# Forming three of thirty-two groups of a tuned matmul with seven block products, in list-scheduled orders

## The chip, the cores and the metric

The kernel runs on one core of one Trainium2 chip. The metric is the device time of one execution in microseconds (us). The engines of the core are TensorE (PE, matmuls; PEld is its weight load), VectorE (DVE), ScalarE (ACT), GpSimd (POOL, which also issues the loads of x) and SyncE (SP, which issues nearly all stores). They run at the same time, each through its own list of instructions in order, and wait for one another by semaphores.

## The reference

```python
B, S, D = (16, 2048, 1024)
def reference(x, w, decay):        # x: B,S,D   w: D,D   decay: D, all float32
    xw = x @ w
    out[:, 0, :] = xw[:, 0, :]
    for t in range(1, S):
        out[:, t, :] = decay[None, :] * out[:, t - 1, :] + xw[:, t, :]
```

A matrix product of 32768 rows, followed by a linear recurrence over time with one decay for each output channel.

## The kernel before

**Tiles.** Time is cut into 64 chunks of 512 steps, two neighbouring chunks make a group of 1024 steps, and the 1024 output channels make 8 blocks of 128. A *tile* is one group and one block of channels; its product lies in PSUM as 128 channels x 1024 steps (two banks), so that the recurrence runs along the free axis. The reduction over 1024 inputs takes 8 steps k, for each of the two chunks: 16 matmuls of 128x512 in bf16 for a tile (line L131). A *slot* is one tile's turn on TensorE; 31 groups give 248 slots, and the last group is done as two chunks of 8 slots each. Three double-bank tiles `ps0` to `ps2` turn over in PSUM; `spare0` and `spare1` are two more banks, and `spare1` holds the squares of the decays.

**Before the product.** GpSimd's queue loads a chunk of x in four quarters as bf16 (`load`, L105, tile `xb`). VectorE transposes it in 32x32 blocks (`turn`, L115, `xw`), and ScalarE reorders it in two halves into the layout that TensorE streams (`part`, L123, `xt`, a ring of 5).

**After the product.** A tile is done in one of two ways. *Unpaired*: VectorE scans all 1024 steps straight out of PSUM (`run`, L221) into `so`. *Paired*: ScalarE copies the tile out of PSUM to `xs` (`copy`, L183) and makes decay times the even steps in `h` (`odd`, L169); GpSimd adds `h` to the odd steps (`join`, L196); VectorE scans only the 512 odd steps, with the squared decay (`scan`, L201); ScalarE makes decay times the odd results (`even`, L169); and GpSimd adds them to the even steps (`fill`, L246). In either case `save` (L250) keeps the last column where the next group continues the sequence, VectorE transposes the result back in 32x32 blocks (`back`, L258, tile `ot`, a ring of 4 that holds four tiles each), and once four tiles are there SyncE stores them (L282).

**Rings and orders.** `so` is a ring of 4 tiles, `xs` of 3, `h` of 4. The order of each engine's instructions is the program's order. For the first 34 slots and the last 20 it is written out by hand in the table `agenda`, a string of steps for each slot (p copy, g odd, z start value, j join, S scan, h even, c fill, k save, B back, T turn, X and Y part, L load). In between, `usual(s)` gives each slot the same pattern, and two of eight tiles are unpaired. In each slot s that is: the copy, odd half, start value and join of tile s if it is paired, the scan of tile s-1 (or of s itself if unpaired), even half, fill and save of s-1, the out-transpose of s-2 or s-1, then the transposes and parts due for later chunks (`later`), and one or two loads.

Of the kernel before, what the change touches and what calls it, by code (L numbers as in the profile page):

```python
# [25 lines left out]
def kernel(  # L26
# [26 lines left out]
    nc = tc.nc  # L53
# [13 lines left out]
    CH = D // 2  # L67
    CR = CH // NQ

    const = ctx.enter_context(tc.tile_pool(name="const", bufs=1))  # L70
# [23 lines left out]
    def ot_tile(nj):  # L94
        return ring(sb, "ot", 4, [128, nj, CR])

# [22 lines left out]
    def part(c, copy, m0, m1, j0=0, j1=NJ):  # L119
        if c not in xt_of:  # L120
            xt_of[c] = ring(sb, "xt", 5, [128, M, 2, TL], BF16)
        src = xw_of[c][:, m0:m1, j0:j1].rearrange("p m j i e -> p m e (j i)")
        pin(copy(out=xt_of[c][:, m0:m1, :, j0 * P:j1 * P], in_=src))  # L123
# [17 lines left out]
    class Tile:  # L141
# [3 lines left out]
        def __init__(self, g, n, ps, outlets):  # L145
            self.b, self.t0 = chunks[g[0]]
            self.T = TL * len(g)
            self.n, self.ps, self.outlets = n, ps, outlets
            self.paired = n % R != R - 1
            if len(tiles) in flips or len(tiles) - len(slots) in flips:  # L150
                self.paired = not self.paired
            self.turn = len(tiles)
            self.lot = sum(t.paired for t in tiles)
            self.prev = None if self.t0 == 0 else last[n]
            if self.t0 + self.T < S:
                last[n] = const.tile([128, 1], FP32, name=f"keep{n}", bufs=2)
                self.keep = last[n]
            else:
                self.keep = None

        @property
        def so(self):
            if not hasattr(self, "held"):
                self.held = sb.tile([128, 2 * TL + 2], FP32, name=f"so{self.turn % 4}")
            return self.held

        def decayed(self, src):
            h = ring(sb, "h", 4, [128, TL])[:, 0:self.T // 2]
            pin(nc.scalar.activation(  # L169
                out=h, in_=src, func=mybir.ActivationFunctionType.Copy,  # L170
                scale=dec[:, self.n:self.n + 1]))
            return h
# [8 lines left out]
        def copy(self):  # L181
            self.xs = sb.tile([128, 2 * TL], FP32, name=f"xs{self.lot % 3}")[:, 0:self.T]
            pin(nc.scalar.copy(out=self.xs, in_=self.ps))  # L183

        def odd(self):
            self.g = self.decayed(self.ps[:, 0:self.T:2])

        def zero(self):
            if self.prev is None:
                pin(nc.gpsimd.memset(self.so[:, 1:2], 0.0))  # L190
# [3 lines left out]
        def join(self):  # L194
            odds = self.xs[:, 1:self.T:2]
            pin(nc.gpsimd.tensor_tensor(out=odds, in0=self.g, in1=odds, op=ALU.add))  # L196

        def scan(self):
            T, n, so = self.T, self.n, self.so
            if self.paired:  # L200
                pin(nc.vector.tensor_tensor_scan(  # L201
                    out=so[:, 3:T + 2:2],
                    data0=squares[-1][:, n:n + 1].to_broadcast([128, T // 2]),
                    data1=self.xs[:, 1:T:2],
                    initial=0.0 if self.prev is None else self.prev,
                    op0=ALU.mult,
# [8 lines left out]
        def run(self, ps, t, size):  # L215
# [3 lines left out]
            else:  # L219
                before = 0.0 if self.prev is None else self.prev  # L220
            pin(nc.vector.tensor_tensor_scan(  # L221
# [12 lines left out]
        def complete(self):  # L234
            if self.paired:
                self.even()
                self.fill()
            if self.keep is not None:
                self.save()

        def even(self):
            self.h = self.decayed(self.so[:, 1:self.T + 1:2])

        def fill(self):
            T = self.T
            pin(nc.gpsimd.tensor_tensor(  # L246
                out=self.so[:, 2:T + 2:2], in0=self.h, in1=self.xs[:, 0:T:2], op=ALU.add))

        def save(self):
            pin(nc.scalar.copy(out=self.keep, in_=self.so[:, self.T + 1:self.T + 2]))  # L250

# [14 lines left out]
    class Outlet:  # L266


        def __init__(self, ns, nj, half=0, queues=(nc.sync,), pieces=1):
            self.pieces = pieces  # L270
            self.ns, self.missing, self.half = ns, set(ns), half
            self.nj, self.t0, self.queues = nj, half * nj * P, queues
            self.ot = ot_tile(nj)

# [133 lines left out]
    def turn_and_load(c):  # L408
# [60 lines left out]
        20: "Y7 S19 L c16 k17 h17 T8 k19 L c17",  # L469
        21: "p20 g20 L S18 X8 j20 B17 B19",  # L470
        22: "L h18 p21 c18 B16 k18 g21 B18 Y8 z20 L j21 S20",
        23: "p22 z21 z22 S21 L h20 g22 T9 c20 h21",
        24: "k21 k20 j22 S23 X9 L c21 Y9 B20 L",
        25: "B23 k23 p24 B21 g24 z24 j24 S22 z25",
        26: "p25 T10 k22 h22 g25 c22 S24 X10 j25",
        27: "B22 p26 S25 g26 z26 Y10 j26",
        28: "S27 h25 h24 c25 S26 c24",
# [26 lines left out]
    flips = (1, 13, 15, -19, -18, -11, -8, -6, -3, -2)  # L504
    later = {}
    begun = {"T": 12, "X": 11, "Y": 11}
    for c in range(5, nch):
        first = c // 2 * K
        ahead = (7, 6, 4) if c % 2 else (11, 10, 8)
        for letter, a in zip("TXY", ahead):  # L510
            if c >= begun[letter]:
                later.setdefault(first - a, []).append(f"{letter}{c}")

    def usual(s):
        paired = [t.paired for t in tiles]
        do = [f"P{s}"] if paired[s] else []
        if paired[s - 1]:
            do.append(f"S{s - 1}")
        if not paired[s]:
            do.append(f"S{s}")  # L520
        do.append(f"C{s - 1}")
        if paired[s - 2]:
            do.append(f"B{s - 2}")
        if not paired[s - 1]:
            do.append(f"B{s - 1}")
        return do + later.get(s, []) + ["L"] * (2 if len(loads) > NQ else 1)

    def rest(s):
        do = [f"S{s - 1}"] if tiles[s - 1].paired else []
        do.append(f"C{s - 1}")  # L530
        if tiles[s - 2].paired:
            do.append(f"B{s - 2}")
        return do + [f"B{s - 1}"] + later.get(s, []) + ["L"] * len(loads)

    def perform(do):
        for deed in do:
            deeds[deed[0]](int(deed[1:] or 0))

    perform(agenda[-99].split())
    spares = [spare] + [ring(psp, "spare1", 1, [128, TL])]  # L540
    for step, (g, n) in enumerate(slots):
        T = TL * len(g)
        left = step - len(slots)
        if n % R == 0:
            ns, nj = range(n, n + R), T // P
            both = -6 * R <= left < -2 * R
            outlets = [Outlet(ns, nj, queues=(nc.sync, nc.gpsimd) if both else (nc.sync,),
                              pieces=2 if left == -2 * R else 1)]
        if left == -R:
# [52 lines left out]
        tiles.append(Tile(g, n, ps, outlets))  # L602
        do = agenda.get(step, agenda.get(left) if left >= -20 else None)
        if do is None:
            do = usual(step)
        else:
            do = do.split()
            if left == -20:
                do = rest(step) + do
        perform(do)  # L610
    assert not loads
# [28 lines left out]
```

## Time and profile before

| | us |
|---|---|
| median of 3 runs | 908.76 (908.70 to 909.01) |
| span of the profiled execution | 907.2 |
| busy: PE, DVE, ACT, POOL | 892.8, 826.3, 686.2, 663.0 |
| loads of x: issue to landing | 7.8 (median) |
| stores of 512 KB: issue to landing | 10.9 (median) |
| mean granted TensorE clock | 0.998 |

The profile shows one execution on the chip. Its span runs from the first to the last instruction; the time of a run also has what lies around the span, and no time of the profiled execution itself is recorded, so that the runs' median stands beside the span here. Busy times are sums over an engine's instructions; matmuls are pipelined and overlap in the records. "L131" is a line of the kernel, an arrow points from the operands to the output (`ot<-so`), buffer numbers are left out, and "x15" counts instructions.

### The profile page before, as it was taken

Reading aid. Unit: us, or ns where it says so; the run is one execution under the profiler, and the core shown is the slowest. Engines: PE = TensorE matmul, PEld = TensorE weight load, DVE = VectorE, ACT = ScalarE, POOL = GpSimd, SP = SyncE. Lnnn points to the kernel's source line nnn. Section 1 sums busy time; section 2 is a strip of 40 time slices with the busy share of each in tenths; the row PEclk is TensorE's granted clock in tenths of the full one; section 3 lists DMA queues with packets and bytes.
Section 4 is the critical chain, followed back from the end, with each engine's and each line's share of the span. In section 5 each row is a group of like instructions: output and inputs, shape, how many; then the busy total and the mean of one; then the engine's idle time right before and its main releaser. Section 6 shows DMA issues by size and latency. Waiting matters only on the chain.

```text
span 907.2 us, 12004 instructions
## 1 busy us (share of the span) xinstructions
PE 892.8 (98%) x4119; PEld 411.4 (45%) x4201; DVE 826.3 (91%) x628; ACT 686.2 (76%) x955; POOL 663.0 (73%) x763
## 2 busy tenths in 40 slices
PE   9999999999999999999999999999999999999996
PEld 5444444444444444444444444444444444444443
DVE  4999989999999999899999999999999999999996
ACT  4889867777777877877877778778778778777742
POOL 7888678877777767768677777777677686776562
PEclk9999999999999999999999999999999999999999
DMA  9999999999999999999999999999999999999788
GB/s 194 194 215 220 227 215 220 215 238 255 249 250 254 241 243 259 247 244 228 227 233 227 227 232 227 226 232 233 220 230 231 228 231 223 232 229 207 153 161 211
DMA packets 397230, 204.77 MB, mean 226 GB/s; under 512 B 8816, under 2 KB 395376, under 8 KB 397168
## 3 DMA queue, kind: packets, MB, share of 16 engines
q1 hardware_dynamic: 258960, 131.62, 59.6%
q0 software_dynamic: 137920, 71.85, 58.1%
q8 instruction: 33, 0.54, 0.2%
q10 hardware_dynamic: 288, 0.52, 0.2%
q14 instruction: 29, 0.24, 0.1%
HBM read 138.42 MB, written 134.22 MB: 301 GB/s over the span
## 4 chain that ended last, share of the span: by engine, by line
PE 93%; DMA 2%; POOL 1%; issue 1%; DVE 1%; ACT 0%; POOLq 0%; DVEq 0%
PE ps L131 93%; DMA xb<-in_x_dram 2%; POOL ot L299 1%; POOL xb L105 1%; PE spare L131 1%; DVE xw L115 0%; ACT xt L123 0%; ACT xs L183 0%; DVE so L201 0%; PE spare L387 0%; DVE ot L258 0%; ACT h L169 0%; PE ps L387 0%; POOLq L635 0%; POOL xs L196 0%
## 5 line engine op out<-in xcount | busy, mean ns | idle before, releaser
L131 PE MATMUL ps<-xt,wsb 128*128 128x512 bf16 x3942 | 863.5, 378 | 4.7 <-ACT h L169 0.2
L131 PEld LDWEIGHTS <-wsb 128*128 128x128 bf16 x4152 | 405.9, 98 | 479.9 <-ACT wsb L306 0.8
L196 POOL TENSOR_TENSOR xs<-h,xs 128x512 f32<-128x512 f32 (+1 forms) x190 | 243.0, 1279 | 181.8 <-ACT h L169 79.4
L183 ACT COPY xs<-ps 128x1024 f32<-128x1024 f32 (+1 forms) x190 | 189.4, 997 | 155.3 <-PE ps L131 144.2
L258 DVE STREAM_TRANSPOSE ot<-so 128x1024 f32<-128x1024 f32 (+1 forms) x260 | 300.1, 1191 | 2.1 <-POOL so L190 1.1
L246 POOL TENSOR_TENSOR so<-h,xs 128x512 f32<-128x512 f32 (+1 forms) x190 | 241.4, 1272 | 39.0 <-ACT h L169 25.7
L123 ACT COPY xt<-xw 128x2048 bf16<-128x2048 bf16 (+1 forms) x136 | 242.3, 1790 | 7.8 <-DVE xw L115 7.6
L105 POOL DMA_DIRECT2D xb<-in_x_dram x264 | 174.3, 661 | 3.3 <-DMA ot<-in_w_dram 1.1
L169 ACT ACTIVATE h<-so,dec 128x512 f32<-128x512 f32 (+1 forms) x190 | 145.4, 766 | 27.7 <-DVE so L201 24.4
L115 DVE STREAM_TRANSPOSE xw<-xb 128x2048 f32<-128x2048 f32 (+1 forms) x78 | 147.4, 1901 | 5.5 <-DMA xb<-in_x_dram 5.5
L201 DVE TENSOR_TENSOR_SCAN so<-spare,keep,xs 128x512 f32<-128x512 f32 (+1 forms) x97 | 120.0, 1239 | 27.7 <-POOL xs L196 27.4
L201 DVE TENSOR_TENSOR_SCAN so<-spare,xs 128x512 f32<-128x512 f32 x93 | 113.3, 1220 | 27.6 <-POOL xs L196 24.6
L169 ACT ACTIVATE h<-ps,dec 128x512 f32<-128x512 f32 (+1 forms) x190 | 130.3, 686 | 0.0
L221 DVE TENSOR_TENSOR_SCAN so<-dec,ps 128x1024 f32<-128x1024 f32 x34 | 76.8, 2261 | 1.0 <-ACT h L169 1.0
L221 DVE TENSOR_TENSOR_SCAN so<-dec,keep,ps 128x1024 f32<-128x1024 f32 (+1 forms) x35 | 75.9, 2169 | 0.1
L250 ACT COPY keep<-so 128x1 f32<-128x1 f32 x136 | 25.3, 189 | 9.9 <-DVE so L221 9.4
L192 ACT COPY so<-keep 128x1 f32<-128x1 f32 x97 | 18.4, 191 | 2.6 <-DVE ot L258 2.4
L131 PE MATMUL ps<-xw,wsb 128*128 128x256 bf16 (+1 forms) x68 | 11.2, 301 | 0.1
L190 POOL MEMSET so<- 128x1 f32 x93 | 10.7, 117 | 0.6 <-DVE ot L258 0.6
L131 PE MATMUL spare<-xt,wsb 128*128 128x512 bf16 (+1 forms) x48 | 10.0, 335 | 0.0
L282 POOL DMA_DIRECT2D out_dram<-ot x8 | 5.7, 722 | 5.5 <-DVE ot L258 5.1
L299 POOL DMA_DIRECT2D ot<-in_w_dram x12 | 6.6, 546 | 3.3 <-DMA xb<-in_x_dram 2.0
(38 smaller groups left out, 44.5 us busy)
## 6 DMA issues: line engine op xcount, KB each, us to landing
out_dram<-ot SPq DMA_DIRECT2D x244, 512.0 KB, 10.9
xb<-in_x_dram POOLq DMA_DIRECT2D x248, 256.0 KB, 7.8
xb<-in_x_dram POOLq DMA_DIRECT2D x16, 128.0 KB, 5.8
out_dram<-ot POOLq DMA_DIRECT2D x4, 512.0 KB, 11.6
ot<-in_w_dram POOLq DMA_DIRECT2D x12, 128.0 KB, 5.1
out_dram<-ot SPq DMA_DIRECT2D x4, 256.0 KB
out_dram<-ot POOLq DMA_DIRECT2D x4, 256.0 KB, 8.5
out_dram<-ot SPq DMA_DIRECT2D x8, 128.0 KB, 4.3
```

The costliest lines, as they stand in the source:

```text
L105: pin(nc.gpsimd.dma_start(out=xb_of[c][quad(q), j0:j1], in_=_ap(x, [[D, P], [P * D, j1 - j0], [1, CQ]], (b * S + t0 + j0 * P) * D + q * CQ)))
L115: pin(nc.vector.transpose(out=dst.rearrange("p (m j i) -> p j m i", m=M, i=P)[:, j0:j1, m0:m1], in_=src.rearrange("p (j m c) -> p j m c", ...
L123: pin(copy(out=xt_of[c][:, m0:m1, :, j0 * P:j1 * P], in_=src))
L131: pin(nc.tensor.matmul(out=ps[:, t0:t1] if ps.shape[1] >= t1 else ps, lhsT=lhs, rhs=rhs, start=(k == 0 and t0 == start), stop=(k == K - 1),))
L169: pin(nc.scalar.activation(out=h, in_=src, func=mybir.ActivationFunctionType.Copy, scale=dec[:, self.n:self.n + 1]))
L183: pin(nc.scalar.copy(out=self.xs, in_=self.ps))
L196: pin(nc.gpsimd.tensor_tensor(out=odds, in0=self.g, in1=odds, op=ALU.add))
L201: pin(nc.vector.tensor_tensor_scan(out=so[:, 3:T + 2:2], data0=squares[-1][:, n:n + 1].to_broadcast([128, T // 2]), data1=self.xs[:, 1:T:2 ...
L221: pin(nc.vector.tensor_tensor_scan(out=so[:, t + 2:t + 2 + size], data0=dec[:, n:n + 1].to_broadcast([128, size]), data1=ps, initial=befor ...
L246: pin(nc.gpsimd.tensor_tensor(out=self.so[:, 2:T + 2:2], in0=self.h, in1=self.xs[:, 0:T:2], op=ALU.add))
L250: pin(nc.scalar.copy(out=self.keep, in_=self.so[:, self.T + 1:self.T + 2]))
L258: pin(nc.vector.transpose(out=outlet.ot[:, :, c0:c0 + P], in_=self.so[:, 2 + t0:2 + t0 + nj * P].rearrange("p (i t) -> p i t", t=P)))
```

## The change

Groups 8, 16 and 24 no longer form each tile by sixteen matmuls. Their 1024 steps are two chunks a and b, their 1024 inputs two halves, and two neighbouring blocks of channels n0 and n1 make the other side: a product of 2x2 blocks, done with seven block products of 4 matmuls each in place of eight (Strassen's identity, in a form with shared sums). For a group, VectorE and GpSimd in turn make four sums of 128x2048 in bf16 (three in a new tile `sx`, one in place in `xt`); the differences of weight blocks are made once, by VectorE, in 20 instructions of 128x512 in bf16 (`wd`). The products of a pair of tiles accumulate in the two banks `a` and `b` of one `ps` tile and in `spare0` (`c`). As one product serves several results, ScalarE copies the state of a bank out to `so` between products (`lift`, four of 128x512 a pair), and VectorE adds or subtracts a bank to what lies there (`join`, three of 128x512 a pair); TensorE's next product into that bank waits for them. Every tile of these groups is paired, and its `odd` step reads `so` in SBUF and not PSUM.

The orders of slots 34 to 243 are no longer made by `usual`: `steady` describes each instruction of these slots as a job with an engine, a cost, a key (its due time) and the jobs it comes after, and `in_order` emits them by list scheduling: whenever an engine is free, the ready job with the smallest key. The jobs are performed in the order of their planned starts, which fixes each engine's list. Which tiles are unpaired there is set by `SHARE` by the distance from a changed group: 32 tiles in slots 34 to 243. `turn` is issued in two halves there.

`xs` goes: the PSUM copy writes into `so`, and join, scan and fill work in place, so `so` is one ring of 7. The rings of `ot` and `xt` shrink from 4 and 5 to 3 and 4; in `agenda` X8, Y8, X9, Y9, X10 and Y10 move later or leave it. First and last slots are otherwise as before.

```diff
+    OTS, XTS, SOS, HS = 3, 4, 7, 4
+    FROM, TO = 34, 244
+    SUMS, SUMT = ('dve', 'pool', 'dve', 'pool'), -20
+    WBY, WLEAD, WSTEP = "dve", 90, 2
+    SHARE = {-1: 0.33, 0: 0, 1: 0.2, 2: 0.16, 3: 0.14, 9: 0.14}
+    merged = (8, 16, 24)
...
-            xt_of[c] = ring(sb, "xt", 5, [128, M, 2, TL], BF16)
+            xt_of[c] = ring(sb, "xt", XTS, [128, M, 2, TL], BF16)
...
-                self.held = sb.tile([128, 2 * TL + 2], FP32, name=f"so{self.turn % 4}")
+                self.held = sb.tile([128, 2 * TL + 2], FP32, name=f"so{self.turn % SOS}")
...
         def copy(self):
-            self.xs = sb.tile([128, 2 * TL], FP32, name=f"xs{self.lot % 3}")[:, 0:self.T]
-            pin(nc.scalar.copy(out=self.xs, in_=self.ps))
+            pin(nc.scalar.copy(out=self.line, in_=self.ps))
...
+    def differ(d, j):
+        k1, n1, k2, n2 = differences[d]
+        one, two = (wsb[:, k * R:(k + 1) * R, n + 2 * j].rearrange("p k q i -> p k (q i)")
+                    for k, n in ((k1, n1), (k2, n2)))
+        by = nc.vector if WBY == "dve" else nc.gpsimd
+        pin(by.tensor_tensor(out=wd[:, d, j], in0=one, in1=two, op=ALU.subtract))
...
+        def product(out, xs, ws, begin):
+            for k in range(R):
+                pin(nc.tensor.matmul(out=out, lhsT=ws(k), rhs=xs[:, k // 2, k % 2],
+                                     start=begin and k == 0, stop=k == R - 1,
+                                     skip_group_check=True))
...
+            def sums(i, engine):
...
+                a, b = xt_of[c0], xt_of[c1]
+                S1, S2, S0 = (sx[0][:, k] for k in range(3))
+                out, one, two = ((S1, b[:, 0:2], b[:, 2:4]), (S2, a[:, 0:2], S1),
+                                 (S0, a[:, 2:4], S2), (b[:, 0:2], a[:, 0:2], b[:, 0:2]))[i]
...
+                pin(engine.tensor_tensor(out=flat(out), in0=flat(one), in1=flat(two), op=ALU.add))
...
+            what = {
+                "a1": ("a", lambda: S(0), w_at(0, n0), True, 0),
+                "a2": ("a", lambda: S(1), w_less(1), False, 3),
+                "b1": ("b", lambda: S(2), w_at(1, n1), True, 4),
+                "c": ("c", lambda: xb_()[:, 2:4], w_less(4), True, 5),
+                "a3": ("a", lambda: xa()[:, 0:2], w_less(2), False, 6),
+                "b2": ("b", lambda: xa()[:, 2:4], w_less(0), False, 8),
+                "a4": ("a", lambda: xb_()[:, 0:2], w_less(3), False, 9),
+            }
...
+            a1 = mult("a1", done + weights + (after_ps[bank - 3] if bank >= 3 else []))
+            A1 = lift(0, 1, "a", at("a1"), [a1, gone[0]])
+            a2 = mult("a2", [A1])
+            A2 = lift(0, 0, "a", at("a2"), [a2, gone[0]])
+            b1 = mult("b1", [a1])
+            B1 = lift(1, 0, "b", at("b1"), [b1, gone[1]])
+            c = mult("c", [after_spare[0], part_of[c1, 1]])
+            C = join(0, 1, "c", ALU.add, at("c"), [c, A1])
...
+            a3 = mult("a3", [A2])
+            A3 = join(1, 0, "a", ALU.subtract, at("a3"), [a3, B1])
+            b2 = mult("b2", [B1])
+            B2 = join(0, 0, "b", ALU.subtract, at("b2"), [b2, A2], True)
+            a4 = mult("a4", [A3])
+            A4 = lift(1, 1, "a", at("a4"), [a4, gone[1]])
...
+        if FROM <= step < TO:
+            if step == FROM:
+                steady(outlets)
+            continue
...
-        do = agenda.get(step, agenda.get(left) if left >= -20 else None)
-        if do is None:
-            do = usual(step)
...
+        perform(agenda.get(step, agenda.get(left)).split())
```

In `what` each product has a bank, a moving block, weights, whether it is the first in its bank, and its due time in products. In the changed kernel's numbering the joins stand at L822, the lifts at L816, the sums at L758, the differences at L614, the products at L741 and the ordinary matmuls at L138; the paired tile's PSUM copy is L197, `odd` and `even` L184, GpSimd's two additions L211 and L261, the scans L216 and L236, and `back` L273.

## The prediction

> **What bounds the kernel now.** I read the page's engine totals and its chain of waits first, then TensorE's own waits, the stretches, and last the groups of instructions with shapes kept apart.
>
> From the page, the busy times of the engines and the chain that ended last:
>
> ```profile
> PE 892.8 (98%) x4119; PEld 411.4 (45%) x4201; DVE 826.3 (91%) x628; ACT 686.2 (76%) x955; POOL 663.0 (73%) x763
> ...
> PE 93%; DMA 2%; POOL 1%; issue 1%; DVE 1%; ACT 0%; POOLq 0%; DVEq 0%
> ```
>
> TensorE (PE) carries the end, and VectorE (DVE) comes next with 91%. TensorE's waits and one unbroken piece of its timeline (start, length, line, count):
>
> ```profile
> PE ps L131 <- ACT h L169: 0.2, 1, 0.2
> PE ps L131 <- DVE wsb L306: 0.2, 1, 0.2
> ```
>
> ```profile
> 884.66 3.40 PE L131 MATMUL ps<-xt,wsb 128*128 128x512 bf16 x15
> ```
>
> Matmuls overlap (one lasts 379 ns), so the pitch is (3.40 - 0.38) / 14 = 0.2157 us. The x@w work is 4096 matmuls of 512 columns: 4096 x 0.2157 = 883.5 us, and TensorE works on them from 10.9 to 896.7 us. Hardly a microsecond of waiting is left between, so only fewer matmuls can shorten this kernel, and every later wait of TensorE is a loss.
>
> Two stretches (length, then busy us of PE, PEld, DVE, ACT, POOL; granted clock):
>
> ```profile
> 70.00:120.00 50.00, 49.74 (x229) 22.64 (x232) 49.87 (x37) 44.55 (x60) 37.96 (x43) 1.00 1.23 222
> 400.00:500.00 100.00, 99.53 (x456) 45.30 (x463) 92.60 (x66) 76.67 (x105) 75.10 (x86) 1.00 1.19 229
> ```
>
> Until 120 us VectorE has no gap; in the steady part it is 92.6% busy. Counting back 3424 + 128 pitches from 896.7 us, slot 34, where the new orders begin, starts near 130 us. The groups of instructions with shapes apart (count | busy us, mean ns | idle before):
>
> ```profile
> L258 DVE STREAM_TRANSPOSE ot<-so 128x1024 f32<-128x1024 f32 x248 | 292.4, 1216 | 2.0 <-POOL so L190 1.1 <-POOL so L246 0.3
> L196 POOL TENSOR_TENSOR xs<-h,xs 128x512 f32<-128x512 f32 x183 | 237.8, 1299 | 175.2 <-ACT h L169 75.9 <-issue 53.7 <-ACT so L192 40.6
> L246 POOL TENSOR_TENSOR so<-h,xs 128x512 f32<-128x512 f32 x183 | 236.2, 1292 | 33.7 <-ACT h L169 22.5 <-ACT keep L250 8.9 <-ACT so L192 2.1
> L183 ACT COPY xs<-ps 128x1024 f32<-128x1024 f32 x183 | 185.3, 1012 | 151.6 <-PE ps L131 141.4 <-remote 5.7 <-POOL so L246 3.4
> L169 ACT ACTIVATE h<-so,dec 128x512 f32<-128x512 f32 x183 | 141.7, 775 | 21.6 <-DVE so L201 18.3
> L115 DVE STREAM_TRANSPOSE xw<-xb 128x2048 f32<-128x2048 f32 x62 | 141.7, 2285 | 0.6 <-DMA xb<-in_x_dram 0.6
> L169 ACT ACTIVATE h<-ps,dec 128x512 f32<-128x512 f32 x183 | 126.9, 694 | 0.0
> L201 DVE TENSOR_TENSOR_SCAN so<-spare,xs 128x512 f32<-128x512 f32 x93 | 113.3, 1220 | 27.6 <-POOL xs L196 24.6
> L221 DVE TENSOR_TENSOR_SCAN so<-dec,ps 128x1024 f32<-128x1024 f32 x34 | 76.8, 2261 | 1.0 <-ACT h L169 1.0
> L196 POOL TENSOR_TENSOR xs<-h,xs 128x256 f32<-128x256 f32 x7 | 5.2, 744 | 6.6 <-ACT h L169 3.5 <-ACT so L192 3.1
> L183 ACT COPY xs<-ps 128x512 f32<-128x512 f32 x7 | 4.1, 585 | 3.7 <-PE ps L131 2.9 <-POOL so L246 0.7
> L306 DVE COPY wsb<-ot 128x512 bf16<-128x512 bf16 x7 | 1.9, 332 | 2.6 <-DMA ot<-in_w_dram 2.6
> L391 DVE COPY xb<-ps 128x512 f32<-128x512 f32 x1 | 0.7, 692 | 0.0
> ```
>
> These give the price of one tile: paired, VectorE pays a half-length scan (about 1.25) and GpSimd (POOL) and ScalarE (ACT) the rest; unpaired, VectorE alone pays about 2.29.
>
> **TensorE's part.** A group of 8 tiles is 128 matmuls now; by seven products for eight it is 112. Three groups: 48 matmuls less, -48 x 0.2157 = -10.4 us. The built programs bear this out (48 matmuls and 48 weight loads fewer), so that the change does not do what it says is no rival here. Each product is the same 512-column matmul with a weight load of its own, so the pitch stays.
>
> **VectorE's part, by group.** An ordinary group lasts 128 x 0.2157 = 27.6 us. VectorE's rows for it: 8 out-transposes x 1.216 = 9.7, two chunk transposes x 2.285 = 4.6, six half scans x 1.25 = 7.5, two full x 2.29 = 4.6; together 26.4. The stretch shows 92.6% of 27.6 = 25.6, because neighbours overlap slightly; so I take rows times 0.97. In the new orders the share of unpaired tiles falls to one or two of eight (32 of slots 34 to 243, where it was one in four), so VectorE needs 24.6 with one and 25.6 with two, and gains 3.0 or 2.0 us on TensorE in each ordinary group. Splitting the chunk transpose in two costs some 0.1 each, nothing beside this.
>
> A changed group lasts 24.2 us. VectorE's rows: 9.7 + 4.6 + eight half scans 10.0 + twelve joins out of PSUM (the 692 ns copy out of PSUM is the nearest row) 8.3 + two bf16 sums of 2048. The trace has no bf16 sum: four times the 332 ns bf16 copy gives 1.3, the 2048-element transpose 2.29; I take 1.3, nearer in type. Sum 35.2 x 0.97 = 34.1: VectorE falls 10.0 us behind in each changed group. The seven ordinary groups between give back 3 x 2 + 4 x 3 = 18, so it catches up.
>
> May it fall behind? A tile's copy L183 waits for the out-transpose of the tile 7 earlier. In a changed group 7 tiles last 7 x 3.02 = 21.1 us, and copy, odd half, join, scan, even half, fill and transpose last 1.01 + 0.69 + 1.30 + 1.25 + 0.78 + 1.29 + 1.22 = 7.5. So 13.6 us of lag is covered; 10.0 fits, with 3.6 to spare. If that cover goes, every further microsecond is one of TensorE.
>
> The 20 weight differences stand in VectorE's order between the scans of tiles 34 and 39, in blocks of up to six: 20 x 0.4 = 8 us, between 0.33 (the copy) and 0.69 (the fp32 copy of 512). Groups 4 to 7 have 3 + 3 + 2 + 2 = 10 us of slack, so 2 are left when group 8 begins. Queued behind a block are the half scans, for which ScalarE's L169 and then its PSUM copies wait.
>
> **The other engines.** About 20 tiles become paired: GpSimd +20 x 2.59 = 52 us, plus six sums. A sum of 2048 there, on the line through the 256 and 512 rows, is 1.299 + 6 x 0.555 = 4.6 us, six make 28: 663 + 80 = 743 of about 897, or 83%. ScalarE: 20 x 2.48 = 50, and 48 half copies x 0.585 = 28 for 24 copies x 1.012 = 24: 740, also 83%. Neither is the bound over all; in a changed group GpSimd needs 8 x 2.59 + 5.3 of DMA issues + 9.2 = 35 of 24.2 us, but has far more than 10 us of slack before it. The sums' chain (1.3 + 4.6 + 1.3 + 4.6 = 12 us) starts about 14 us ahead of the group by the order, and only the last product kind needs its last link: cost nothing, or up to 2 us a group if it slips. The rings cut to 3 (stores land 10.9 us after issue, the ring turns in 3 x 13.8) and 4 cost nothing.
>
> **Waits inside a changed group.** Here TensorE waits for half copies on ScalarE and joins on VectorE within one pair of tiles. Between first and last join VectorE's order holds 12 joins, 5 half scans, 5 out-transposes and half a chunk transpose: 8.3 + 6.25 + 6.1 + 1.2 = 21.8, x 0.97 = 21.2. TensorE's time from the end of the first c product (12 matmuls, 2.6 us in) to the last product (0.9) is 24.2 - 3.5 = 20.7, and TensorE's order has 12 matmuls of the next tile (2.6 us) before that last product. So it just fits, if GpSimd delivers the scans' inputs in time. I take 1.2 us a group, 3.6 in all, between 0 and 3 each.
>
> **The rivals.** (1) All waits are hidden: the full 10.4, 898.4 us. For it: TensorE's waits are 0.4 us now, and the orders are planned from durations close to these rows. Against: VectorE has nothing to spare in the changed groups.
>
> (2) Slower: VectorE's lag outgrows the seven-tile ring. The differences and sums are the only frequent VectorE instructions with two tensors in SBUF (scans take squares or inputs from PSUM); no row shows how they fare beside GpSimd's tensor operations, which fill 6 x 2.59 / 27.6 = 56% of the time. If each waits for the operation under way, that is 0.56 x 0.65 = 0.36 us on average, 1.3 at worst; the fp32 rate adds 0.29. For the 20 differences: 7.2 + 5.8 = 13 us, for the two sums of group 8 some 3.3. Lag at its end: 13 - 2 + 10 + 3.3 = 24.3, less 13.6 = 10.7 us of TensorE, and 908.8 - 10.4 + 3.6 + 10.7 = 912.7. At 1.3 each it passes 930. With one of the two, about 6.5: 6.5 - 2 + 10 + 1.6 - 13.6 = 2.5, or 904.5. It makes the change a loss from about 9 us, 0.45 a difference, on.
>
> [...]
>
> (3) The fixed orders miss in ordinary groups, ScalarE's above all (one unpaired tile: 26.5 of 27.6 us by rows): 0.6 us in each of 23 groups is 14 us, 912. Against: slack grows back everywhere.
>
> **How the numbers follow.** The execution's span is 907.2; the median of the runs, 908.76, is 1.6 more, which I keep. Forecast: 907.2 + 1.6 - 10.4 + 3.6 + 1.5 (rival 2's middle between 0 and 2.5) = 903.5, chance 0.56, own range 899.5 to 906.5. Rival 1: 0.16. Rival 2 in full: 0.15, rival 3: 0.05, both slower. Between, within 0.2% (1.8 us, about what a measurement of this kernel can tell): 0.08. Faster 0.72, same 0.08, slower 0.20. The range reaches from rival 1 to just past no change, 898.4 to 911.0, leaving out most of rivals 2 and 3.
>
> **What would show it.** Right: 48 matmuls fewer, TensorE waiting 1 to 2 us near each of the three changed groups on L816 and L822, VectorE without a gap in groups 8 to 13. Rival 2: L614 near or above 0.7 us or gaps before it, and TensorE's longest waits in groups 5 to 8. Rival 3: TensorE waits spread over ordinary groups on L197 and L184. I am wrong if the three groups cost more than 10 us of waits with L614 at 0.4.

## The result: 951.5 us, 4.7% slower

The changed kernel takes 951.53 us (median of 4 runs, 950.81 to 952.45) against 908.88 before: 1.0469 times, interval 1.0454 to 1.0484, or 42.6 us more where 5.3 less were forecast. The profiled execution has a span of 948.9 us against 907.2.

The page of the changed kernel, engine totals and chain of waits:

```profile
PE 893.8 (94%) x4072; PEld 407.9 (43%) x4153; DVE 838.6 (88%) x742; ACT 730.4 (77%) x1049; POOL 741.4 (78%) x825
...
PE 31%; DMA 19%; DVE 16%; issue 7%; POOL 7%; SPq 7%; ACT 5%; DVEq 0%; POOLq 0%; ACTq 0%
```

TensorE held 93% of the chain before and holds 31% now; transfers come next, though no transfer was added. TensorE's sum can be closed. The 48 matmuls are gone, so its busy time should be 892.8 - 10.4 = 882.4 us; it is 893.8, 11.4 more. TensorE worked for 17.7 us at a granted clock of 0.5, which makes 8.9 of them; the rest is about what the records add at breaks (a matmul overlaps the next by 0.16 us, and there are 18 more breaks). Its idle time is 948.9 - 893.8 = 55.1 us against 907.2 - 892.8 = 14.4 before, 40.7 more. -10.4 + 11.4 + 40.7 = 41.7, the difference of the spans.

Where the idle time lies (gaps of over 0.25 us in TensorE's timeline after 100 us, 42.1 us in all; there was none before): 11.7 us at slot 34, where the new orders begin (142 to 175 us), 19.9 us in three stops at 381, 448 and 652 us, only 6.0 us in the three changed groups, and 4.6 us after 870 us. TensorE's timeline at slot 34 and at two of the later stops (start, length, count; in brackets the wait before):

```profile
142.13 7.07 PE L138 MATMUL ps<-xt,wsb 128*128 128x512 bf16 x31 [1.90 <-ACT h L184]
155.07 5.05 PE L138 MATMUL ps<-xt,wsb 128*128 128x512 bf16 x16 [5.87 <-ACT h L184]
...
174.75 15.44 PE L138 MATMUL ps<-xt,wsb 128*128 128x512 bf16 x62 [3.91 <-ACT h L184]
...
447.82 36.52 PE L138 MATMUL ps<-xt,wsb 128*128 128x512 bf16 x157 [11.15 <-ACT h L184]
...
652.15 48.19 PE L138 MATMUL ps<-xt,wsb 128*128 128x512 bf16 x209 [6.68 <-ACT h L184]
```

All of these are in ordinary groups, and all end with ScalarE's `odd` (L184), which frees a PSUM tile. ScalarE only passes the wait on. The waits of all engines (total, times, longest):

```profile
ACT h L184 <- DVE so L216: 105.2, 70, 10.9
...
DVE ot L273 <- DMA out_dram<-ot: 35.7, 10, 12.0
PE ps L138 <- ACT h L184: 32.6, 8, 11.2
POOL xb L112 <- DVE xw L122: 30.0, 9, 12.7
...
DVE xw L122 <- DMA xb<-in_x_dram: 13.5, 7, 3.3
...
PE ps L741 <- ACT so L816: 4.9, 8, 0.9
```

Read from the bottom up: VectorE stands before transposes of x that have not landed and, for longer, before an `ot` tile whose store has not landed; GpSimd stands before loads whose `xb` VectorE has not emptied; ScalarE's `even` waits for VectorE's scans, its copies out of PSUM queue behind, and TensorE waits for a bank. Before, stores landed 10.9 us after issue and loads 7.8; the DMA issues now (count, KB, median us to landing):

```profile
out_dram<-ot SPq DMA_DIRECT2D x244, 512.0 KB, 13.4
xb<-in_x_dram POOLq DMA_DIRECT2D x248, 256.0 KB, 10.4
```

VectorE's timeline at slot 34 and just ahead of the stop at 448 us:

```profile
149.24 1.25 DVE L122 STREAM_TRANSPOSE xw<-xb 128x1024 f32<-128x1024 f32 x1 [2.95 <-DMA xb<-in_x_dram]
...
439.45 1.25 DVE L273 STREAM_TRANSPOSE ot<-so 128x1024 f32<-128x1024 f32 x1 [11.99 <-DMA out_dram<-ot]
```

The second line leads to the largest single loss: 12 us of VectorE, and 11.15 us of TensorE that end 8 us later. The stops at 381 and 652 us each have such a wait for a store ahead of them too, of 6.3 us.

### The profile page after: what moved, and what is told of

It reads as the page before. It is cut to its first block, busy times and chain, and to the rows that moved or that the text cites. A ratio compares the mean times of both kernels' runs of the same rounds, so it can differ in the third digit from the quotient of the medians.

```text
span 948.9 us, 11992 instructions
## 1 busy us (share of the span) xinstructions
PE 893.8 (94%) x4072; PEld 407.9 (43%) x4153; DVE 838.6 (88%) x742; ACT 730.4 (77%) x1049; POOL 741.4 (78%) x825
## 4 chain that ended last, share of the span: by engine, by line
PE 31%; DMA 19%; DVE 16%; issue 7%; POOL 7%; SPq 7%; ACT 5%; DVEq 0%; POOLq 0%; ACTq 0%
PE ps L138 24%; DMA out_dram<-ot 14%; SPq L302 7%; PE ps L741 6%; DVE ot L273 5%; DMA xb<-in_x_dram 5%; DVE so L216 5%; DVE xw L122 4%; POOL so L211 3%; POOL so L261 3%; ACT h L184 2%; POOL xb L112 1%; ACT xt L130 1%; ACT so L816 1%; DVE so L236 1%
## 5 line engine op out<-in xcount | busy, mean ns | idle before, releaser
L138 PE MATMUL ps<-xt,wsb 128*128 128x512 bf16 x3565 | 792.0, 381 | 40.1 <-ACT h L184 32.6
L138 PEld LDWEIGHTS <-wsb 128*128 128x128 bf16 x3768 | 370.2, 98 | 478.4 <-issue 50.4
L273 DVE STREAM_TRANSPOSE ot<-so 128x1024 f32<-128x1024 f32 (+1 forms) x260 | 305.5, 1194 | 54.4 <-DMA out_dram<-ot 35.7
L261 POOL TENSOR_TENSOR so<-h,so 128x512 f32<-128x512 f32 (+1 forms) x211 | 270.1, 1287 | 105.9 <-ACT h L184 77.9
L211 POOL TENSOR_TENSOR so<-h,so 128x512 f32<-128x512 f32 (+1 forms) x211 | 270.9, 1288 | 48.2 <-ACT h L184 39.0
L184 ACT ACTIVATE h<-so,dec 128x512 f32<-128x512 f32 (+1 forms) x235 | 178.3, 768 | 106.1 <-DVE so L216 105.2
L197 ACT COPY so<-ps 128x1024 f32<-128x1024 f32 (+1 forms) x187 | 186.3, 996 | 61.8 <-PE ps L138 57.7
L122 DVE STREAM_TRANSPOSE xw<-xb 128x1024 f32<-128x1024 f32 (+2 forms) x130 | 153.2, 1195 | 14.4 <-DMA xb<-in_x_dram 13.5
L216 DVE TENSOR_TENSOR_SCAN so<-spare,so 128x512 f32<-128x512 f32 x107 | 126.8, 1197 | 7.0 <-POOL so L211 5.5
L184 ACT ACTIVATE h<-ps,dec 128x512 f32<-128x512 f32 (+1 forms) x187 | 128.1, 685 | 0.4 <-POOL so L261 0.4
L216 DVE TENSOR_TENSOR_SCAN so<-spare,keep,so 128x512 f32<-128x512 f32 (+1 forms) x104 | 125.6, 1219 | 0.8 <-POOL so L211 0.7
L236 DVE TENSOR_TENSOR_SCAN so<-dec,keep,ps 128x1024 f32<-128x1024 f32 (+1 forms) x28 | 59.6, 2128 | 4.2 <-PE ps L138 4.0
L236 DVE TENSOR_TENSOR_SCAN so<-dec,ps 128x1024 f32<-128x1024 f32 x20 | 45.1, 2258 | 2.9 <-PE ps L138 2.9
L741 PEld LDWEIGHTS <-wd 128*128 128x128 bf16 x240 | 23.2, 98 | 36.0 <-issue 5.3
L741 PE MATMUL ps<-xt,wd 128*128 128x512 bf16 x142 | 35.0, 379 | 2.8 <-ACT so L816 2.2
L816 ACT COPY so<-ps 128x512 f32<-128x512 f32 x48 | 27.0, 587 | 12.5 <-PE ps L741 10.5
L741 PE MATMUL ps<-sx,wsb 128*128 128x512 bf16 x92 | 23.6, 379 | 0.8 <-DVE so L236 0.6
L741 PE MATMUL ps<-sx,wd 128*128 128x512 bf16 x48 | 12.4, 380 | 2.7 <-ACT so L816 2.6
## 6 DMA issues: line engine op xcount, KB each, us to landing
xb<-in_x_dram POOLq DMA_DIRECT2D x248, 256.0 KB, 10.4
out_dram<-ot POOLq DMA_DIRECT2D x4, 512.0 KB, 11.6
```

Of the source, the lines that this page charges most:

```text
L122: pin(nc.vector.transpose(out=dst.rearrange("p (m j i) -> p j m i", m=M, i=P)[:, j0:j1, m0:m1], in_=src.rearrange("p (j m c) -> p j m c", ...
L138: pin(nc.tensor.matmul(out=ps[:, t0:t1] if ps.shape[1] >= t1 else ps, lhsT=lhs, rhs=rhs, start=(k == 0 and t0 == start), stop=(k == K - 1),))
L184: pin(nc.scalar.activation(out=h, in_=src, func=mybir.ActivationFunctionType.Copy, scale=dec[:, self.n:self.n + 1]))
L197: pin(nc.scalar.copy(out=self.line, in_=self.ps))
L216: pin(nc.vector.tensor_tensor_scan(out=so[:, 3:T + 2:2], data0=squares[-1][:, n:n + 1].to_broadcast([128, T // 2]), data1=so[:, 3:T + 2:2] ...
L236: pin(nc.vector.tensor_tensor_scan(out=so[:, t + 2:t + 2 + size], data0=dec[:, n:n + 1].to_broadcast([128, size]), data1=ps, initial=befor ...
```

## The experiments

**Are the products or the orders at fault?** e1 keeps the new orders, rings and `steady`, and forms no group by products.

```diff
-    merged = (8, 16, 24)
+    merged = ()
```

> The list-scheduled orders and the smaller rings without any changed group (all 4096 matmuls, no sums, differences, lifts, joins). Theory A (the new orders issue the loads of x in bursts; stores then land up to 19.7 us after issue, and VectorE, with a ring of 3 ot tiles, stands waiting for them): the bursts are still there, so TensorE still idles near slot 34 and at one to three later places, 925 to 950 us. Theory B (the block products' own work on VectorE is what TensorE waits for): without it nothing is left to wait for, 907 to 912 us.

925.9 us (1.0190, interval 1.0160 to 1.0219). 17 of the 42.6 us come with the orders alone, nearly all at slot 34: gaps of 1.9, 6.3 and 2.5 us at 142, 155 and 164 us, then none over 0.25 us up to 886. VectorE waits for no store here. The stops at 381, 448 and 652 us need the changed groups.

e4 is e1 with the ring of `ot` back at 4:

```diff
-    OTS, XTS, SOS, HS = 3, 4, 7, 4
+    OTS, XTS, SOS, HS = 4, 4, 7, 4
```

> As e1 (orders without any changed group), with the ot ring back at 4. Theory A: the waits for stores go, the idle time near slot 34 (GpSimd's queue full of loads, not the ring) stays: 912 to 925 us. Theory B: as e1 within 2 us, 907 to 912. If the ring of 3 alone is the cause and not the bursts: 907 to 912 here and 925 to 950 in e1.

924.2 (1.0171, 1.0142 to 1.0201). The small gap at 142 us is gone, the two large ones at slot 34 stay, at 6.2 and 2.6: they are not the ring's. With the changed groups a ring of 4 was not run, so its part in the three later stops is not known.

**Loads.** The planner issues each load as soon as `xb` is free by its reckoning, four at a time. In e2 it keeps 2.6 us between planned loads; e7 and e6 are the same edit with 2.0 and 1.1, e5 with 1.1 for chunks 12 to 14 alone.

```diff
-                got = [Job("pool", cost["L"], need - 28 + 2.5 * q, lambda c=c, q=q: load(c, q),
-                           [turned.get(c - 3)]) for q in quads]
+                got = []
+                for q in quads:
+                    got.append(Job("pool", cost["L"], need - 28 + 2.5 * q, lambda c=c, q=q: load(c, q),
+                                   [turned.get(c - 3)] + [(a, 2.6) for a in latest]))
+                    latest[:] = got[-1:]
```

> The changed kernel with one edit: in the planner each load of a quarter chunk may start only 2.6 us after the one before it has been issued, so that loads come about every 3.3 us. Theory A: stores land within about 14 us again, VectorE's waits for stores fall from 35.7 us to under 8, the idle time at slot 34 from 11.9 to under 3 us, and the time to 900 to 910 us. Theory B: no change beyond 5 us, 945 to 955.

981.8 (1.0805, 1.0757 to 1.0853): worse, though VectorE's waits for stores fall to 3.7 us and the three later stops are gone. Now 39 us of gaps lie in the changed groups, which use a chunk every 12 us. In groups 16 and 24 TensorE waits for late parts of x (6.6 us in all) and for the sums made of them (10.7 us). In group 8 it is something else: VectorE's second sum, 1.20 us where nothing is in its way, takes 6.78, while GpSimd makes two additions and a sum of its own without a pause (until 256.75 us). VectorE's sum and TensorE's matmuls behind it:

```profile
251.07 6.78 DVE L762 TENSOR_TENSOR sx<-xt,sx 128x2048 bf16<-128x2048 bf16 x1
...
257.90 3.57 PE L745 MATMUL ps<-sx,wsb 128*128 128x512 bf16 x8 [7.33 <-DVE sx L762]
```

> As e6 with 2.0 us (2.7 us from start to start; a changed group of 24.2 us needs one every 3.0). Theory A2: waits for stores nearly gone as in e2, and unlike e2 no load comes too late for a changed group, 903 to 920 us. If e2's stalls inside the changed groups came from holding loads back at all: 6 us or more of idle per changed group, 930 to 980.

956.7 (1.0521, 1.0468 to 1.0575): 7.3 to 8.2 us are lost at the start of each changed group, each time behind the same sum, which takes 6.79 to 6.87 us beside three GpSimd operations in a row. VectorE's waits for stores are down to 3.1 us.

> As e5 with all loads of the planned slots held 1.1 us apart (about 1.8 us from start to start, which a changed group can keep up with, where e2's 3.3 could not). Theory A1 + A2 (after a changed group VectorE is behind, chunks are freed in clumps, loads come in clumps, stores land late and the ring of 3 ot tiles stops VectorE): stores land in 11 to 12 us, the waits for stores fall under 12 us, 905 to 925 us. If the clumping is not what slows the stores: as e5, 930 to 940.

931.7 (two runs, 926.9 and 936.4; 1.0246, 1.0121 to 1.0371). Some 20 us are back (15 to 25 by the two runs): the three later stops are gone, none of the gaps between 180 and 880 us is over 1.4. VectorE's waits for stores fall from 35.7 to 20.7 us, and GpSimd no longer stands before a load until VectorE has emptied its tile. At slot 34 gaps of 9.3 us stay. Two waits of e6, to be held against 105.2 and 35.7:

```profile
ACT h L184 <- DVE so L216: 58.5, 56, 6.5
...
DVE ot L273 <- DMA out_dram<-ot: 20.7, 12, 5.6
```

> The changed kernel with the twelve loads of chunks 12 to 14, which the new orders issue in one burst at slot 34, held 1.1 us apart (start to start about 1.8 us); every other load as in the changed kernel. Theory A1 (the burst fills the eight DMA semaphores of GpSimd's queue, GpSimd stands behind its own loads, and its additions come late): the 11.7 us of idle TensorE at slots 34 to 46 and some 5 us of half clock there go, the later stalls on stores stay, 932 to 938 us. If the slot-34 stall has another cause (the weight differences on VectorE): idle there stays above 8 us, 945 to 952.

954.3 (1.0495, 1.0465 to 1.0525): the spacing has to hold throughout, and slot 34 does not mind it (gaps of 11.6 us there).

e8 is the edit of e5 without changed groups:

```diff
-    merged = (8, 16, 24)
+    merged = ()
...
+                                   [turned.get(c - 3)] + [(a, 1.1 if c <= 14 else 0) for a in latest]))
```

> e1 (orders without any changed group) with e5's edit. Theory A1: the idle time at slots 34 to 46, 10.7 us in e1 and all that e1 had beside its tail, goes: 908 to 911 us. If the weight differences or anything else of the changed groups mattered there, e1 could not have had it; if the hand-over of the orders itself costs, 915 to 926.

926.9 (1.0193, 1.0155 to 1.0231), as e1; one gap of 7.6 us in place of 6.3 and 2.5. Its VectorE timeline shows why: earlier loads hardly hold GpSimd up any more (1.2 us of waits, 8.0 in e1), and VectorE waits all the longer for those of chunk 12.

```profile
150.98 2.37 DVE L122 STREAM_TRANSPOSE xw<-xb 128x1024 f32<-128x1024 f32 x2 [8.29 <-DMA xb<-in_x_dram]
```

**Other landing times for the planner.** e3 tells it that loads land after 14 and stores after 20 us.

```diff
-    LAND = 9.0
-    STORED = 13.0
+    LAND = 14.0
+    STORED = 20.0
```

> The changed kernel with two constants of the planner: a load lands 14 us after issue (9 before) and a store 20 us (13 before); bursts are not forbidden. Theory A: VectorE's list then has other work in front of an instruction that waits for a transfer, but the transfers stay as slow: 910 to 935 us. Theory B: within 5 us of 951.

948.4 (1.0437, 1.0407 to 1.0468): 3 us. The stop at 448 halves to 5.1; the gaps at slot 34 are 12.6 us.

**Earlier loads.** e9 adds six loads (`L`; its expectation says seven) to slots 27 to 31 of `agenda`; e10 does so without changed groups; e11 adds the spacing of 1.1 us to e9, and e12 to that landing times of 12 and 16.

```diff
-        27: "B22 p26 S25 g26 z26 j26",
-        28: "S27 h25 h24 c25 S26 c24",
+        27: "B22 p26 S25 g26 z26 L j26",
+        28: "S27 h25 h24 L c25 S26 c24 L",
...
```

> The changed kernel, but the hand-written slots 27 to 31 issue seven loads more, so that chunk 12 and most of chunk 13 are on their way before slot 34. Theory A3 (VectorE's list puts the transpose of chunk 12 in front of tile 34's scan, because the planner lets a load issued at its time zero land 9 us later; issued late and landing after 11 to 12 us, it stops VectorE, then ScalarE, then TensorE): the 11.7 us of idle at slots 34 to 46 and the half clock behind it go, the three later stalls stay, 930 to 938 us. If the hand-over stall has another cause: above 945.

> e1 (orders without any changed group) with the same earlier loads. Theory A3: the hand-over was all that the orders cost, 908 to 912 us. Otherwise 920 or more.

> e9's earlier loads and e6's 1.1 us between loads together, with the three changed groups. Theories A3 + A2: both stalls gone, what stays is about 2 us of waits in each changed group and some 3 us at the end of the planned slots: 903 to 913 us. If the two causes are not separate, as e6: 920 to 935.

> As e11 with the planner's landings nearer to the measured ones (12 us for a load, 16 for a store). Theory A2: VectorE's list keeps other work in front of what waits for a transfer, up to 3 us better than e11: 901 to 911 us. If landings no longer matter once loads are held apart: e11 within 1.5 us.

952.9 (1.0485), 921.3 (1.0136), 926.2 (1.0189) and 931.7 (1.0253). Little is won (4.6 us in e10 against e1), since a stop now lies ahead of slot 34: the stores of the hand-written slots meet more loads, and VectorE waits for one of them. The VectorE timeline of e10:

```profile
131.18 1.25 DVE L273 STREAM_TRANSPOSE ot<-so 128x1024 f32<-128x1024 f32 x1 [6.50 <-DMA out_dram<-ot]
```

**What happens at slot 34.** The loads of chunk 12 are the last ones that `agenda` issues (slots 32 and 33), so `chunk(12)` finds none left to plan (e5 and e8 space the eight of chunks 13 and 14, not twelve): `got` is empty, and with it the list `ends`, which carries `LAND`. The transpose of chunk 12 has no landing time at all, and the plan sets its first half 7.2 us after the start (5.9 in e1), ahead of tile 34's scan. That is cause (a), and no value of `LAND` reaches it. Cause (b) stands in GpSimd's order, ahead of tile 34's `join`: the next loads, and in the program each load waits for the one eight loads earlier (in the changed kernel's trace the one at 142.06 us starts 0.28 us after that one has landed). GpSimd's timeline in e1:

```profile
137.12 3.84 POOL L112 DMA_DIRECT2D xb<-in_x_dram  x6
...
144.12 0.67 POOL L112 DMA_DIRECT2D xb<-in_x_dram  x1 [0.42 <-DMA xb<-in_x_dram]
146.59 0.65 POOL L112 DMA_DIRECT2D xb<-in_x_dram  x1 [1.80 <-DMA xb<-in_x_dram]
149.04 0.64 POOL L112 DMA_DIRECT2D xb<-in_x_dram  x1 [1.80 <-DMA xb<-in_x_dram]
...
149.72 1.30 POOL L211 TENSOR_TENSOR so<-h,so 128x512 f32<-128x512 f32 x1
```

e13 takes (a) away without changed groups, e14 (a) and, with the first loads 2.6 us apart, (b).

```diff
-                ends = [(a, LAND) for a in got]
+                ends = [(a, LAND) for a in got] + ([(place[FROM - 1, "S"], 16)] if c == 12 else [])
...
+                                   [turned.get(c - 3)] + [(a, 2.6 if c <= 14 else 0) for a in latest]))
```

> No changed groups; chunk 12's transpose is planned 16 us after the scan of tile 33 or later, where the plan had it 7 us in, since no landing was counted for loads issued before slot 34. Theory (a), the uncounted landing: VectorE no longer waits for xb ahead of tile 34's scan; of the idle 13.3 us of the orders alone the two later gaps (6.3 and 2.5) go, with some 4 us lost at half clock: 925.9 - 12 = about 914. Rival (b), loads in GpSimd's order: each still holds an addition up by 1.8 us, the gaps shrink by 2 at most, 922 to 925. Rival (c), the orders' start out of step: the gap of 1.9 at 142 stays or grows, 918 or more.

928.3 (1.0220, 1.0204 to 1.0235). No gain: VectorE waits as long, now for GpSimd's addition (the scan's wait below), and TensorE's gap at 156 us is 6.6.

```profile
151.98 2.50 DVE L216 TENSOR_TENSOR_SCAN so<-spare,so 128x512 f32<-128x512 f32 x2 [6.47 <-POOL so L205]
```

> As the run before, and the planned loads of chunks 12 to 14 at least 2.6 us apart. Theory (a) alone: no difference to the run before, about 914. If (b) holds besides: 3 to 5 us better than the run before, since GpSimd then never stands before a load. What idle time is left near slot 34 is (c), 2 us if only the gap at 142.

927.6 (1.0218, 1.0198 to 1.0239). The time is the same, but the gaps at slot 34 fall from 10.7 us in e1 to 2.9. So (a) and (b) ran side by side to the same 150 us, each enough alone: e8 removed (b) and left (a) with 8.29 us, e13 removed (a) and left (b) with 6.47, and e14 removed both. The time is lost again in new places (3.8 us at 252, 2.2 at 312): six loads go out back to back from 214.7 to 217.9 us, and ahead of the first of these stops VectorE waits 5.6 us for a store. In all it waits 37.8 us for stores here.

**Both repairs with the changed groups.** e15 is the changed kernel with the edit of chunk 12, e16 with all loads 1.1 us apart as well.

```diff
+                                   [turned.get(c - 3)] + [(a, 1.1) for a in latest]))
...
+                ends = [(a, LAND) for a in got] + ([(place[FROM - 1, "S"], 16)] if c == 12 else [])
```

> The changed kernel with the one edit of chunk 12's transpose. Theory (a): the hand-over loses its 9.8 us of later gaps and some 4 at half clock, and the later stalls of clumped loads stay: about 951.5 - 13 = 938. Rival (b) or (c): 947 to 951. A third case: the shifted plan clumps the loads in another way, and the later stalls move or change by 10 us either way.

> The edit of chunk 12's transpose, and all planned loads at least 1.1 us apart. If the hand-over and the clumped loads are the two causes and add up: 931.7 - 12 = 916 to 921, within 1.3% of the time before. Rival: (b) or (c) keep the hand-over at 9 us and more: 928 to 932.

947.6 (1.0430, 1.0415 to 1.0446) and 920.0 (1.0120, 1.0105 to 1.0135). Alone the first repair brings 4 us; on top of the spacing it brings 12 (7 to 16 by e6's two runs), and the spacing on top of it 28.

e17 adds a third: at slot 34 TensorE is some 1.75 tiles ahead of the other engines (in e14 tile 36's matmuls end 4.3 us, or 20 matmuls, after tile 33's scan begins), and the planner starts all engines together. e18 is e17 without changed groups.

```diff
-                last_one = Job("pe", each, t + q * each, do,
+                last_one = Job("pe", each * {FROM: 0.0, FROM + 1: 0.25}.get(s, 1), t + q * each, do,
...
+                                   [turned.get(c - 3)] + [(a, 1.0) for a in latest]))
...
+                ends = [(a, LAND) for a in got] + ([(place[FROM - 1, "S"], 13)] if c == 12 else [])
```

> Changed groups; chunk 12's transpose planned 13 us after tile 33's scan or later, all planned loads at least 1.0 us apart, and the planner told that TensorE is 1.75 tiles ahead at slot 34 (tile 34's products cost nothing, tile 35's a quarter). If the orders' start out of step is the rest of the hand-over: its idle time falls from 6.3 us (the run with transpose and spacing) to 2 or less and the time from 920 to 911 to 915. Rival: the differences, which stand in VectorE's order there and took 11 us, hold it up whatever the planner takes TensorE for: 917 to 922.

> The same three edits without changed groups. If repaired orders run as well as those before, about 910 to 914, and the difference to the run with changed groups is 48 matmuls (10.4 us) less some 6 us of waits in the three groups: 4 us in favour of the changed groups or nothing. If the orders go on to stall elsewhere as in the run with transpose and first loads: 918 to 926, and the difference is 5 us or more.

914.1 (1.0062, 1.0047 to 1.0077) and 915.8 (1.0085, 1.0068 to 1.0102). The engine totals, e17's and then e18's:

```profile
PE 886.7 (97%) x4072; PEld 406.6 (45%) x4153; DVE 844.8 (93%) x742; ACT 730.7 (80%) x1049; POOL 740.7 (81%) x825
```

```profile
PE 893.8 (98%) x4119; PEld 411.0 (45%) x4201; DVE 799.7 (88%) x680; ACT 732.2 (80%) x1040; POOL 720.9 (79%) x822
```

Against the first versions of each (951.5 and 925.9), 37 of 42.6 us and 10 of 17 have been won back. No version beats the kernel before. The two give the changed groups' own worth: TensorE is 7.1 us less busy (10.4, less 2.3 at half clock and about 1 at breaks) and 6.6 us more idle; that leaves 0.5 us by the spans and 1.7 by the medians. The runs overlap (913.8 to 915.8 and 914.6 to 918.2), so that even here a gain is not told from none. Slot 34 in e17 still has 5.0 us of gaps, 2.5 without changed groups: the rival named in the expectation, VectorE's differences, seems to have a part there. The 20 take 17.2 us in e17, 8 in the forecast. A first block stands ahead of the scans of tiles 34 and 35, a second behind them:

```profile
138.50 6.98 DVE L614 TENSOR_TENSOR wd<-wsb 128x512 bf16<-128x512 bf16 x6
...
149.45 5.28 DVE L614 TENSOR_TENSOR wd<-wsb 128x512 bf16<-128x512 bf16 x6
```

## Why the prediction was wrong

**TensorE's term was right in size.** 48 matmuls less are worth the 10.4 us in the sum above, and the products keep the pitch: twelve in a row take 2.75 us, (2.75 - 0.38) / 11 = 0.215 each.

**Waits inside the changed groups: within the bounds.** 1.7, 1.9 and 2.5 us, 6.0 in all, against 1.2 each, 3.6 in all, and bounds of 0 to 3 each.

**Rival 2 was not the main loss, but half of it is there.** The groups of instructions that it priced, in the changed kernel:

```profile
L614 DVE TENSOR_TENSOR wd<-wsb 128x512 bf16<-128x512 bf16 x20 | 12.7, 682 | 0.0
...
L758 POOL TENSOR_TENSOR sx<-xt,sx 128x2048 bf16<-128x2048 bf16 x3 | 12.2, 4069 | 1.0 <-DVE sx L758 1.0
...
L822 DVE TENSOR_TENSOR so<-so,spare 128x512 f32<-128x512 f32 x12 | 8.0, 669 | 1.4 <-PE spare L741 1.4
L758 DVE TENSOR_TENSOR sx<-xt,sx 128x2048 bf16<-128x2048 bf16 x3 | 6.1, 2044 | 0.0
L758 DVE TENSOR_TENSOR sx<-xt 128x2048 bf16<-128x2048 bf16 x3 | 3.6, 1201 | 0.0
```

Its term for the fp32 rate falls: the sum of 2048 takes 1.20 us with nothing in its way (1.3 in the forecast), and of the 20 differences 16 take 0.38 to 0.42 us (0.4). Its term for waiting beside GpSimd is there: the other 4 take 0.71 to 3.07, 12.7 us for the 20 where 8 were counted. Each of the 4 ends 0.28 to 0.29 us after the GpSimd operation, or the second of two, that it met. The sum made while GpSimd works takes 2.04 us on average. That just one of the two terms would come, on which the 2.5 us behind the forecast's 1.5 stand, was my estimate: no trace of the kernel before shows it. The forecast's "1.3 at worst" was too small: it took VectorE to wait for one GpSimd operation, but the difference of 3.07 us ran beside two additions without a pause between (168.59 to 171.14 us) and ended 0.29 us after the second; in e2 a sum took 6.78 us. The last stop at slot 34, at 175 us, comes behind two such differences (2.27 and 3.07 us), so that a part of that stop is rival 2's; e1, without differences, has gaps of 10.7 us there in place of 11.7. But the sign I gave for it, TensorE waiting in groups 5 to 8 for a ring of seven, did not come: ScalarE's copies wait for matmuls (57.7 us), not for out-transposes. The joins, 0.67 to 0.69 against 0.692, and GpSimd's sums, 4.07 and 4.73 against 4.6, were priced well.

**The step that failed** is the sentence "The rings cut to 3 (stores land 10.9 us after issue, the ring turns in 3 x 13.8) and 4 cost nothing", and beside it that the new orders were given no price where they begin. The second of these is shown by e1: 17 us without any changed group, 10.7 of them gaps at slot 34 and 4.3 half clock behind these. In the first, the landing time is what was wrong. Landing times are no constants of the kernel: the loads' and the stores' share is set by the orders. In the changed kernel, from 400 to 440 us, loads move 103 GB/s and stores 115; between 100 and 120, where the hand-written order spaces the loads, 50 and 190. The same 512 KB land up to 18.5 us after issue in the first stretch and up to 8.5 in the second. The trace of the kernel before had it too, under a median of 10.9: from 150 to 190 us its loads move 105 GB/s and its stores 109, and there the stores land after 18.3 us in the median, the last figure of this row:

```profile
out_dram<-ot SPq DMA_DIRECT2D x10, 512.0 KB, 18.3
```

With its ring of 4 and its order VectorE did not wait for them. A ring that turns in 41 us has room for 20, if its tiles are spread; that VectorE, behind its time, fills them in a bunch until the room is gone is inferred from its waits of up to 12 us, and how much of them the ring of 3 makes is open. The same holds for VectorE, which "gains 3.0 or 2.0 us on TensorE in each ordinary group", "so it catches up": that leaves out its waits for transfers, 35.7 + 13.5 us. Their sum alone is no price, though: in e14, without changed groups, VectorE waits 37.8 us for stores, 8.3 at most at once, and the gaps come to 13.6 us in all.

**Rival 3** had the right place, ordinary groups and fixed orders, with a wrong price and a chance of 0.05. I spread 0.6 us over 23 groups; the orders miss in four places, slot 34 and the three later stops, by 2 to 12 us each, and ScalarE, which I named "above all", only passes the wait on. The point against it, "slack grows back everywhere", is what VectorE, working in its listed order, did not give: its transpose at 439.45 us waited 11.99 us for a store, and everything listed behind it waited too. Half clock after a stop, 8.9 us, was in no term. "I am wrong if the three groups cost more than 10 us of waits" missed too: they cost 6.

**What stays open.** Two things about the later stops were not separated. The ring of 3 and the late stores act together there, since no run has the changed groups with a ring of 4. And the spacing of loads does two things at once: it leaves the stores more of the transfers, and it keeps GpSimd from standing before a load (30.0 us of waits for VectorE, 2.4 in e17). The remaining 5 us of e17 against the kernel before are what slot 34 (gaps of 3.9 and 1.1 us, and half clock behind the first), gaps of 0.3 to 1.9 us elsewhere and the rest leave of the 10.4 us saved; they were not taken apart.

## What to carry to other kernels

Where a planner writes fixed orders, look first at the seam where it takes over: everything under way there (loads issued, engines behind one another) has to be in its starting state, and a missing delay shows as one engine that waits for a transfer ahead of work that was ready. Price a transfer's landing by what else the new order issues in the same 20 us, not by its median in the old one. And when two waits end at the same time, taking either away shows nothing; only both together tell. Look at what GpSimd does beside VectorE's sums and differences, which have two inputs in SBUF: in e2, beside three GpSimd operations in a row, 1.20 us became 6.78.

## What the runs showed of the hardware

In the changed kernel TensorE's granted clock was 0.5 for 3.4 us at its stops of 2.93, 3.91 and 5.87 us, for 6.8 at that of 6.68 and for 10.2 at that of 11.15; at the last three of these it fell while TensorE still stood (at 154.6, 649.5 and 441.3 us). After its stops of 1.90 and 2.03 us it was 1.00. So a longer stop cost more than its length: sixteen matmuls, 15 x 0.2157 + 0.38 = 3.6 us at full clock, took 5.05 us after the gap of 5.87, and 6.14 in e1 after one of 6.30.

VectorE's sums and differences, with two inputs in SBUF, took longer beside GpSimd's additions and sums. The bf16 sum of 128x2048 took 1.20 us in the changed kernel with nothing in its way and 2.04 on average beside GpSimd's work; in e2 it took 1.20 and, beside three GpSimd operations in a row, 6.78. In the changed kernel 16 of the 20 differences took 0.38 to 0.42 us, and the two that met two additions in a row 2.27 and 3.07. The joins, with one input in PSUM, took 0.65 to 0.69 us, though 16 of the 36 lay wholly beside such GpSimd work.
